# A mixture-of-experts kernel on one core: x loaded in float32 by SyncE and cast on the engines, instead of partly cast by Pool's transfer

## The chip, the cores and the metric

The kernel runs on one core of one Trainium2 chip. A core has five engines with their own instruction streams: TensorE (PE; its weight loads are listed as PEld), VectorE (DVE), ScalarE (ACT), GpSimd (POOL) and SyncE (SP). They share an on-chip memory of 128 partitions (SBUF) and the accumulators that TensorE writes (PSUM). Sixteen DMA engines move data between the chip's main memory and SBUF; an instruction on SP's or Pool's queue starts a transfer. The engines wait for one another, and for transfers, through semaphores. The metric is device time in microseconds (us).

## The reference

```python
n_experts, capacity, hidden, expert_hidden = 8, 256, 512, 2048

def reference(x, w1, w2):          # x 8x256x512, w1 8x512x2048, w2 8x2048x512, all float32
    h = np.matmul(x, w1)
    h = np.maximum(h, 0)
    return np.matmul(h, w2).astype(np.float32)
```

Eight experts, each with two matrix products and a ReLU between them. The weights are 67.1 MB in float32, x and the output 4.2 MB each.

## The kernel before

All products are done in bfloat16. The weights are cast while they are loaded: a transfer on Pool's queue reads float32 and writes bfloat16. Four experts' weights fit into SBUF (`w1_sb` and `w2_sb`, four slots each; expert e uses slot e mod 4).

*Loading x.* x is seen as 128 partitions with 16 rows of 512 numbers each: partition 16e + pp holds rows 16pp to 16pp + 15 of expert e. `x_sb`, in bfloat16, lies in slot 2 of `w2_sb`, which no expert needs yet. Rows 0 to 3 of each partition (`HEAD = 4`) are loaded by SP in float32 into the place of the outputs (`out_sb`, free until the first expert is done) and cast into `x_sb` by VectorE (L213 and L214). Rows 4 to 15 are loaded by Pool's first transfer (L153), which casts on the way. After L136 stands the end of a section of the program (L137, L138), where the engines meet; SP's first transfer is issued ahead of it.

*Transposing.* TensorE needs x with the hidden dimension on the partitions. It waits for the cast, for the identity matrix that Pool builds (L154 and L157) and for Pool's part of x (L323 to L325), and transposes 64 blocks of 128 x 128 in four rounds (`transposes`). VectorE and ScalarE copy each round from PSUM into `xT` (L206).

*Pool's queue.* After x and the identity come twelve loads of weights (L190) in the order of `loads`: w1 of experts 0 and 1, w2 of 0 and 1, w1 of 2 and 3, w2 of 2 and 3, and so on, with single experts and halves at the end. The first three are issued at once. The fourth overwrites slot 2, where x lies, and waits for the last transpose (L171). The later ones wait until the expert that had the slot has been computed (L174, L176). The last load is preceded by a tiny transfer into `out` (L181), whose landing tells Pool that the queue has come as far as the last weights; then the outputs of experts 0 to 6 are written by one transfer (L193), and SP writes those of expert 7 (L145). The semaphore `d_pool` counts 16 for x, 16 for the tiny transfer and 16 for the outputs.

*Computing.* SP waits for each load in turn and passes the news to TensorE (L142, L143). For each expert TensorE computes the hidden layer in four groups of 16 matmuls (`h_ps`), ScalarE applies ReLU into `hT` (L239), TensorE computes the outputs (`o_ps`, 32 matmuls), and VectorE copies them to `out_sb` (L225); the last half of expert 7 is copied by ScalarE (L245). TensorE's matmuls all go through one helper and are listed with L275.

Of the kernel before, what the change touches and what calls it, by code (L numbers as in the profile page):

```python
# [16 lines left out]
def kernel(  # L17
# [7 lines left out]
    nc = tc.nc  # L25
    P = 128
    E, C, H = x.shape
    F = w1.shape[2]
    MC = C // P
# [2 lines left out]

    R = E * C // P

    HEAD = 4

    NS = 4

# [10 lines left out]
    x_v = x.rearrange("e (pp r) k -> (e pp) (r k)", r=R)  # L49
# [7 lines left out]
    def allot(name, shape, dtype):  # L57
        nonlocal free
        places[name] = free
        t = nc.alloc_sbuf_tensor_at(name, shape, dtype, offset=free)  # L60
        free += math.prod(shape[1:]) * mybir.dt.size(dtype)
        return t


    out_sb = allot("out_sb", [P, E, MC, H], FP32)
# [7 lines left out]
    x_sb = w2_sb[:, 2, :]  # L73
# [8 lines left out]
    def sem(name):  # L82
        s = nc.alloc_semaphore(name)
        sems.append(s)
        return s

    d_last, d_pool = sem("d_last"), sem("d_pool")
# [3 lines left out]
        for w, slots in [(1, (0, 2, 3)), (2, (0, 1, 2, 3))]  # L91
        for i in slots
    }
    d_head, d_half = sem("d_head"), sem("d_half")
    s_event, s_cast, s_stored = sem("s_event"), sem("s_cast"), sem("s_stored")
    s_pe, v_last = sem("s_pe"), sem("v_last")

# [3 lines left out]
    def after_transposes(n):  # L101
        return s_pe, n

    def after_hidden(e, groups):
        return s_pe, K1 * MC + e * (NG + MC) + groups

    def after_outputs(e, halves):
        return s_pe, K1 * MC + e * (NG + MC) + NG + halves
# [22 lines left out]

    x_head = out_sb[:, :HEAD // MC].rearrange("p e m h -> p (e m h)")
    with tc.tile_critical(no_gpsimd_drain=True):
        nc.sync.dma_start(x_head, x_v[:, :HEAD * H]).then_inc(d_head, 16)  # L136
    tc.close()  # L137
    tc.compile()  # L138

# [1 line left out]
    for i, (w, es, h, n) in enumerate(loads):  # L141
# [8 lines left out]


    pool = nc.gpsimd
    pool.dma_start(x_sb[:, HEAD * H:], x_v[:, HEAD * H:]).then_inc(d_pool, 16)  # L153
    pool.memset(identity[:], 0.0).then_inc(s_event)  # L154
    pool.wait_ge(s_event, 1)

# [6 lines left out]
        pattern=[[-1, P]],  # L163
        channel_multiplier=1,
    ).then_inc(s_event)
    for i, (w, es, h, n) in enumerate(loads):


        old = es[-1] - NS
        if w == 2 and 2 in es:  # L170
            pool.wait_ge(*after_transposes(K1 * MC))  # L171
        if old >= 0 and h == 0:
            if w == 1:
                pool.wait_ge(*after_hidden(old, NG))  # L174
            else:
                pool.wait_ge(*after_outputs(old, MC))  # L176
        if i == len(loads) - 1:


            pool.wait_ge(s_event, 3)  # L180
            pool.dma_start(  # L181
                out_v[:16, 0, :16], out_sb[:16, 0, 0, :16]
            ).then_inc(d_pool, 16)
        e, ne, at_slot = es[0], len(es), es[0] % NS
        if w == 2:
            src = w2_v[:, e:e + ne, h:h + n, :].rearrange("p e h n -> p e (h n)")
            dst = w2_sb[:, at_slot:at_slot + ne, h * JH * H:(h + n) * JH * H]
        else:
            src, dst = w1_v[:, e:e + ne, :], w1_sb[:, at_slot:at_slot + ne, :]
        pool.dma_start(dst, src).then_inc(landed[i][0], 16)  # L190
    pool.wait_ge(s_event, 4)
    pool.wait_ge(d_pool, 32)
    pool.dma_start(  # L193
        out_v[:, :E - 1, :], out_sb[:, :E - 1].rearrange("p e m h -> p e (m h)")
    ).then_inc(d_pool, 16)
    pool.wait_ge(s_stored, 1)
    pool.wait_ge(d_pool, 48)
    used = [s.num for s in sems[1:]]
    used = range(min(used), max(used) + 1)
    pool.dma_reset(used)  # L200
# [9 lines left out]


    dve = nc.vector
    dve.wait_ge(d_head, 16)  # L213
    dve.tensor_copy(x_sb[:, :HEAD * H], x_head).then_inc(s_cast)  # L214
    dve.sem_inc(c_xt[0], 1)
    for ko in range(K1):
        dve.wait_ge(*after_transposes(ko * MC + 1))
# [11 lines left out]


    act = nc.scalar
    act.sem_inc(c_xt[1], 1)
    for ko in range(K1):
        act.wait_ge(*after_transposes(ko * MC + 2))
# [15 lines left out]
    pe = nc.tensor  # L250
# [42 lines left out]
    def last_column(step):  # L293

        return (P - 1) * step * 2
# [24 lines left out]
                i += 1  # L320
            t.then_inc(s_pe)

    pe.wait_ge(s_cast, 1)  # L323
    pe.wait_ge(s_event, 2)
    pe.wait_ge(d_pool, 16)  # L325
    x_first = X_AT + last_column(K1)
    pe.reg_mov(reg["x"], x_first)
    loop("transposes", reg["x"], x_first + K1 * 2, transposes)
# [146 lines left out]
```

## Time and profile before

| | |
|---|---|
| runs | 179.47 us median of 3 (179.31 to 180.14) |
| the profiled execution | 180.34 us in all, span 179.0 us |
| mean granted TensorE clock | 0.941 |
| read from main memory, written | 71.30 MB, 4.20 MB |
| transfers on Pool's queue | 38.80 MB at the destination |
| transfers on SP's queue | 1.57 MB |

The span goes from the first to the last instruction of one profiled execution; its own time in all is a little longer. In the lists, "x16" is a number of instructions, an arrow `a<-b` reads "a is written from b", times are in microseconds from the start of the span (the first number is the start, the second the length), and the bracket at the end tells how long the engine had been idle and what ended that. Bytes are counted at the destination, so a transfer that casts float32 to bfloat16 counts half of what it reads. The letter q after an engine's name marks its instruction queue, where transfers are issued and semaphores awaited. Transfers are listed with the time from issue to landing, that is, until the semaphore has its full count.

### The profile page before, as it was taken

How to read it: one execution, taken by the hardware profiler on the slowest of the kernel's cores; microseconds unless marked ns; L12 is line 12 of the kernel's file. 1: busy time of each engine (PE TensorE's matmuls, PEld its weight loads, DVE VectorE, ACT ScalarE, POOL GpSimd, SP SyncE). 2: the span in 40 equal slices, each digit the busy share in tenths (PEclk: the TensorE clock that was granted, in tenths of full speed). 3: DMA queues.
4: the chain of work that ended last, by engine and by line, in shares of the span. 5: the costliest groups of instructions: out<-in, count | busy, mean ns of one | idle time of the engine just before them, and what ended most of it. 6: DMA issues, size and time to landing. Idle time of an engine off the chain costs nothing. (4 is left out here: it accounts for less than half of the span.)

```text
span 179.0 us, 2075 instructions
## 1 busy us (share of the span) xinstructions
PE 126.7 (71%) x824; PEld 89.7 (50%) x832; DVE 15.8 (9%) x20; ACT 38.7 (22%) x38; POOL 10.9 (6%) x21
## 2 busy tenths in 40 slices
PE   0007630695029999993059999999999999959980
PEld 0006520585014695593023795695596497449530
DVE  0203420000000200200000200200110020020010
ACT  2002420044000063044000062053044044005310
POOL 3600010000000002101000101100020000001000
PEclk9999999999557999999657999999999999999999
DMA  5999989999999999999999998999999999999997
GB/s 185 253 207 231 227 190 231 227 194 223 231 209 205 227 216 201 231 216 198 231 220 194 231 223 190 231 227 194 223 231 205 209 234 216 198 212 218 303 421 310
DMA packets 3744, 40.37 MB, mean 226 GB/s; under 512 B 288, under 2 KB 288, under 8 KB 1312
## 3 DMA queue, kind: packets, MB, share of 16 engines
q0 software_dynamic: 3456, 38.80, 97.5%
q1 hardware_dynamic: 288, 1.57, 2.4%
HBM read 71.30 MB, written 4.20 MB: 422 GB/s over the span
## 5 line engine op out<-in xcount | busy, mean ns | idle before, releaser
L275 PE MATMUL o_ps<-w_sb,hT 128*128 x248 | 59.8, 396 | 19.6 <-PEq L99 18.8
L275 PE MATMUL h_ps<-xT,w_sb 128*128 x512 | 60.9, 281 | 11.3 <-PEq L99 11.3
L275 PEld LDWEIGHTS h_ps<-xT,w_sb 128*128 x512 | 57.7, 146 | 15.4 <-issue 12.0
L239 ACT ACTIVATE hT<-h_ps 128x1024 bf16<-128x1024 f32 x32 | 32.8, 1024 | 110.2 <-PE h_ps L275 110.2
L275 PEld LDWEIGHTS o_ps<-w_sb,hT 128*128 128x128 bf16 x256 | 25.5, 101 | 51.2 <-issue 24.7
L225 DVE COPY out_sb<-o_ps 128x512 f32<-128x512 f32 x15 | 9.7, 686 | 140.3 <-PE o_ps L275 140.3
L275 PE MATMUL xt_ps<-identity,w_sb 128*128 128x128 bf16 x64 | 7.6, 311 | 16.2 <-PEq L99 16.2
L275 PEld LDWEIGHTS xt_ps<-identity,w_sb 128*128 x64 | 6.5, 146 | 16.9 <-issue 16.9
L190 POOL DMA_DIRECT2D w_sb<-in_w_dram x12 | 8.0, 667 | 104.2 <-PE h_ps L275 56.9
L206 ACT COPY xT<-xt_ps 128x1024 bf16<-128x1024 bf16 x4 | 4.0, 1012 | 17.0 <-PE xt_ps L275 17.0
L206 DVE COPY xT<-xt_ps 128x1024 bf16<-128x1024 bf16 x4 | 4.9, 1224 | 12.2 <-PE xt_ps L275 12.2
L193 POOL DMA_DIRECT2D out_dram<-out_sb x1 | 1.0, 964 | 33.2 <-DMA out_dram<-out_sb 33.2
L245 ACT COPY out_sb<-o_ps 128x512 f32<-128x512 f32 x1 | 0.6, 586 | 5.9 <-PE o_ps L275 5.9
L206 ACT ACT_TABLE_LOAD x1 | 1.3, 1283 | 2.4 <-PEq L138 2.4
L214 DVE CAST w_sb<-out_sb 128x2048 bf16<-128x2048 f32 x1 | 1.2, 1227 | 5.8 <-DMA out_sb<-in_x_dram 5.8
L181 POOL DMA_DIRECT2D out_dram<-out_sb x1 | 0.5, 512 | 14.7 <-DVEq L228 14.7
L153 POOL DMA_DIRECT2D w_sb<-in_x_dram x1 | 0.7, 682 | 2.4 <-POOLq L138 2.4
L157 POOL TENSOR_SCALAR_AFFINE_SELECT identity<-identity 128x128 bf16<-128x128 bf16 x1 | 0.3, 284 | 0.2 <-POOL identity L154 0.2
L154 POOL MEMSET identity<- 128x128 bf16 x1 | 0.2, 224 | 0.0
L459 POOL MEMSET const-float32-0.0<- 128x1 f32 x1 | 0.1, 93 | 0.2 <-issue 0.2
L459 POOL MEMSET const-bfloat16-1.0<- 128x1 bf16 x1 | 0.1, 96 | 0.0
L459 POOL MEMSET const-uint8-127<- 128x1 uint8 x1 | 0.1, 96 | 0.0
(1 smaller groups left out, 0.1 us busy)
## 6 DMA issues: line engine op xcount, KB each, us to landing
w_sb<-in_w_dram POOLq DMA_DIRECT2D x5, 4096.0 KB, 47.1
w_sb<-in_w_dram POOLq DMA_DIRECT2D x5, 2048.0 KB, 51.2
out_dram<-out_sb POOLq DMA_DIRECT2D x1, 3584.0 KB, 12.9
w_sb<-in_w_dram POOLq DMA_DIRECT2D x2, 1024.0 KB, 43.3
w_sb<-in_x_dram POOLq DMA_DIRECT2D x1, 1536.0 KB, 10.6
out_sb<-in_x_dram SPq DMA_DIRECT2D x1, 1024.0 KB, 4.9
out_dram<-out_sb SPq DMA_DIRECT2D x1, 512.0 KB, 4.7
out_dram<-out_sb POOLq DMA_DIRECT2D x1, 1.0 KB, 33.7
```

Source lines behind the costliest of these rows:

```text
L153: pool.dma_start(x_sb[:, HEAD * H:], x_v[:, HEAD * H:]).then_inc(d_pool, 16)
L157: pool.affine_select(out=identity[:], in_=identity[:], compare_op=mybir.AluOpType.not_equal, fill=1.0, base=0, pattern=[[-1, P]], channel_ ...
L181: pool.dma_start(out_v[:16, 0, :16], out_sb[:16, 0, 0, :16]).then_inc(d_pool, 16)
L190: pool.dma_start(dst, src).then_inc(landed[i][0], 16)
L193: pool.dma_start(out_v[:, :E - 1, :], out_sb[:, :E - 1].rearrange("p e m h -> p e (m h)")).then_inc(d_pool, 16)
L206: return copy(xT[:, ko, m].rearrange("k (ep r2) -> k ep r2", r2=R // MC), xt_ps[m][:].rearrange("k r2 ep -> k ep r2"),)
L214: dve.tensor_copy(x_sb[:, :HEAD * H], x_head).then_inc(s_cast)
L225: cp = dve.tensor_copy(out_sb[:, e, m, :], o_ps[m][:])
L239: act.activation(hT[:, g * GJ:(g + 1) * GJ, :].rearrange("p a c -> p (a c)"), h_ps[g % UG][:], mybir.ActivationFunctionType.Relu,).then_in ...
L245: act.copy(out_sb[:, E - 1, 1, :], o_ps[1][:]).then_inc(v_last)
L275: return pe.add_instruction(inst)
L459: nc = _bacc.Bacc("TRN2", target_bir_lowering=False, num_devices=1)
```

## The change

Now SP loads all of x in float32, in three transfers (rows 0 to 3, 4 to 9 and 10 to 15 of each partition), into the place of the outputs, which they fill entirely. VectorE casts the first transfer, the second, and rows 10 to 13 of the third; ScalarE casts rows 14 and 15. Pool's transfer of x is gone; Pool builds the identity and then waits for x's second transfer before it issues the first weights. TensorE waits for four casts instead of one cast and Pool's transfer. `d_pool` counts 16 less.

```diff
-    HEAD = 4
+    HEAD, BODY = 4, 10
...
-    d_head, d_half = sem("d_head"), sem("d_half")
+    d_x, d_half = [sem(f"d_x{i}") for i in range(3)], sem("d_half")
...
-    x_head = out_sb[:, :HEAD // MC].rearrange("p e m h -> p (e m h)")
+    x_f32 = out_sb[:].rearrange("p e m h -> p (e m h)")
+
+    def rows(a, b):
+        return slice(a * H, b * H)
+
     with tc.tile_critical(no_gpsimd_drain=True):
-        nc.sync.dma_start(x_head, x_v[:, :HEAD * H]).then_inc(d_head, 16)
+        for i, (a, b) in enumerate([(0, HEAD), (HEAD, BODY), (BODY, R)]):
+            nc.sync.dma_start(x_f32[:, rows(a, b)], x_v[:, rows(a, b)]).then_inc(d_x[i], 16)
...
     pool = nc.gpsimd
-    pool.dma_start(x_sb[:, HEAD * H:], x_v[:, HEAD * H:]).then_inc(d_pool, 16)
     pool.memset(identity[:], 0.0).then_inc(s_event)
...
+    pool.wait_ge(d_x[1], 16)
     for i, (w, es, h, n) in enumerate(loads):
...
-    pool.wait_ge(d_pool, 32)
+    pool.wait_ge(d_pool, 16)
...
-    pool.wait_ge(d_pool, 48)
+    pool.wait_ge(d_pool, 32)
...
     dve = nc.vector
-    dve.wait_ge(d_head, 16)
-    dve.tensor_copy(x_sb[:, :HEAD * H], x_head).then_inc(s_cast)
+    SPLIT = 14
+
+    def cast(copy, a, b):
+        return copy(x_sb[:, rows(a, b)], x_f32[:, rows(a, b)])
+
+    dve.wait_ge(d_x[0], 16)
+    cast(dve.tensor_copy, 0, HEAD).then_inc(s_cast)
+    dve.wait_ge(d_x[1], 16)
+    cast(dve.tensor_copy, HEAD, BODY).then_inc(s_cast)
+    dve.wait_ge(d_x[2], 16)
+    cast(dve.tensor_copy, BODY, SPLIT).then_inc(s_cast)
...
     act = nc.scalar
+    act.wait_ge(d_x[2], 16)
+    cast(act.copy, SPLIT, R).then_inc(s_cast)
...
-    pe.wait_ge(s_cast, 1)
     pe.wait_ge(s_event, 2)
-    pe.wait_ge(d_pool, 16)
+    pe.wait_ge(s_cast, 4)
```

## The prediction

> **What bounds the kernel now.** First I read the page's busy shares against its slices. The last line below is the busy share of the 16 DMA engines in 40 slices.
>
> ```profile
> span 179.0 us, 2075 instructions
> PE 126.7 (71%) x824; PEld 89.7 (50%) x832; DVE 15.8 (9%) x20; ACT 38.7 (22%) x38; POOL 10.9 (6%) x21
> DMA  5999989999999999999999998999999999999997
> ```
>
> TensorE is idle 29% of the span, while the DMA engines are full from the first slice to the last. So the kernel is one stream of bytes, and the question is what one byte costs in each part of it. The table by stretches says that (last columns: granted clock, DMA share, GB/s arriving at the destination):
>
> ```profile
> 3.00:4.00 1.00, 0.00 (x0) 0.00 (x0) 0.00 (x0) 0.69 (x1) 0.76 (x3) 1.00 0.99 418
> 4.00:5.00 1.00, 0.00 (x0) 0.00 (x0) 0.00 (x0) 0.00 (x0) 0.85 (x2) 1.00 1.16 438
> ...
> 16.00:160.00 144.00, 111.16 (x719) 78.64 (x727) 12.94 (x18) 32.61 (x32) 5.71 (x10) 0.93 1.02 216
> ...
> 169.00:175.00 6.00, 4.67 (x22) 1.94 (x20) 0.69 (x1) 0.59 (x1) 0.00 (x0) 1.00 1.03 423
> 175.00:177.00 2.00, 0.00 (x0) 0.00 (x0) 0.00 (x0) 0.00 (x0) 0.00 (x0) 1.00 1.03 422
> ```
>
> The weights are cast on the way, so 216 GB/s arriving as bfloat16 are 432 GB/s read as float32. SP's plain float32 load of x (3 to 5 us) moves 428, the plain float32 output at the end 423. A float32 byte of the source therefore costs the same, cast or not. Next, the end, from the timeline, with the issues and their time to landing:
>
> ```profile
> 159.41 7.31 PE L275 MATMUL h_ps<-xT,w_sb 128*128 x64 [2.08 <-PEq L99]
> ...
> 166.61 7.07 PE L275 MATMUL o_ps<-w_sb,hT 128*128 x31
> ...
> 173.71 0.59 ACT L245 COPY out_sb<-o_ps 128x512 f32<-128x512 f32 x1 [5.93 <-PE o_ps L275]
> 174.32 0.35 SPq L145 DMA_DIRECT2D out_dram<-out_sb  x1
> ```
>
> ```profile
> out_dram<-out_sb POOLq DMA_DIRECT2D x1, 3584.0 KB, 12.9
> w_sb<-in_x_dram POOLq DMA_DIRECT2D x1, 1536.0 KB, 10.6
> out_sb<-in_x_dram SPq DMA_DIRECT2D x1, 1024.0 KB, 4.9
> out_dram<-out_sb SPq DMA_DIRECT2D x1, 512.0 KB, 4.7
> ```
>
> TensorE waits 2.08 us for the last expert's w1 before its last two stages; from there to the end everything follows the stream, and Pool's outputs (3584 KB, queued behind the last weights) keep the engines full until SP's last 512 KB land. So a microsecond by which the weights' stream starts later is a microsecond at the end, and a microsecond saved on x's computation is nothing. The change touches the first 14 us:
>
> ```profile
> 0.95 0.38 SPq L136 DMA_DIRECT2D out_sb<-in_x_dram  x1
> 2.41 1.28 ACT L206 ACT_TABLE_LOAD   x1 [2.41 <-PEq L138]
> 2.83 0.68 POOL L153 DMA_DIRECT2D w_sb<-in_x_dram  x1 [2.38 <-POOLq L138]
> 3.51 0.22 POOL L154 MEMSET identity<- 128x128 bf16 x1
> 3.97 0.28 POOL L157 TENSOR_SCALAR_AFFINE_SELECT identity<-identity 128x128 bf16<-128x128 bf16 x1 [0.24 <-POOL identity L154]
> 4.41 0.75 POOL L190 DMA_DIRECT2D w_sb<-in_w_dram  x1 [0.15 <-issue]
> 5.15 2.05 POOL L190 DMA_DIRECT2D w_sb<-in_w_dram  x2
> 5.83 1.23 DVE L214 CAST w_sb<-out_sb 128x2048 bf16<-128x2048 f32 x1 [5.83 <-DMA out_sb<-in_x_dram]
> 13.94 1.31 PEld L275 LDWEIGHTS xt_ps<-identity,w_sb 128*128 x13 [13.94 <-issue]
> ```
>
> Two moments are needed more finely, when Pool's x and when the weights begin to move:
>
> ```profile
> 4.60:4.80 0.20, 0.00 (x0) 0.00 (x0) 0.00 (x0) 0.00 (x0) 0.20 (x1) 1.00 0.78 328
> 4.80:5.00 0.20, 0.00 (x0) 0.00 (x0) 0.00 (x0) 0.00 (x0) 0.20 (x1) 1.00 1.95 553
> ...
> 12.20:12.40 0.20, 0.00 (x0) 0.00 (x0) 0.00 (x0) 0.00 (x0) 0.00 (x0) 1.00 0.68 143
> 12.40:12.60 0.20, 0.00 (x0) 0.00 (x0) 0.00 (x0) 0.00 (x0) 0.00 (x0) 1.00 3.51 737
> ```
>
> Packets come in bursts here. Pool's first x packets show at 4.80, where the share leaves 1 and nearly doubles: 1.97 us after its issue began and 1.3 us after it ended (2.83 + 0.68 = 3.51). By 12.5 the next larger burst is the first of w1; it stands right behind x in Pool's queue, so nothing is lost there.
>
> **The change part by part.**
>
> *SP's issues.* The first stays at 0.95. Two more of 0.38 us each put SP 0.76 us later at the barrier of L138, which releases ScalarE at 2.41 and Pool at 2.83, so these go to 3.2 and 3.6 at most. Pool then needs about 0.9 us for the identity, and waits for x until 9.5 (below). Hidden: 0. Without that cover it would be 0.76.
>
> *The bytes of x.* Four rows of 16 (1.05 MB) already come this way and land at 5.83, where VectorE starts. The other twelve (3.15 MB) take 3.15/0.428 = 7.35 us as float32; through Pool they took from about 5.1 to 12.5, 7.4 us. Gain 0.05, taken as 0; with 418 and 438 for the rate it is -0.1 to +0.2. Rows 4 to 10 take 3.67 us and land at 5.83 + 3.67 = 9.50, the last six at 13.18 (before 2.83 + 10.6 = 13.43). Their data end some 0.7 us ahead of the landing (x's head moved until about 5.1), at about 12.45: until then the engines are busy.
>
> *Pool's new wait.* This is the term that counts. Behind it stand all the weights: the first issue can't begin before 9.50, where it stood ready at 4.41. What covers it is the third x transfer, to 12.45. If it starts at once, data flow 2.0 us after the wait, at 11.6, and the cost is 0. But VectorE wakes on the same semaphore and casts six rows. The trace shows what a cast does to an issue beside it:
>
> ```profile
> 5.86:5.88 0.02, 0.02 (x2) 1.00 0.00 0
> ...
> L190 POOL DMA_DIRECT2D w_sb<-in_w_dram x12: 528/555/1333, 4.4 to 131.1; - x12
> ```
>
> Of the two issues that begin at 5.15 one ends at 5.87 (0.72 us), and the next, beside the cast that runs to 7.06, takes 1.33 us, the longest of all twelve, and ends at 7.20, which is 0.14 us after the cast. I read it as held by the cast, its last step done when VectorE lets go. The six-row cast has 3072 elements a partition: 1.23 x 1.5 = 1.84 us, 9.50 to 11.34. The first issue then ends at 11.48, and its data start 1.3 us later, at 12.8; by the end of x's burst instead of its start (about 5.4 instead of 4.80) 1.9 us later, at 13.4. Against 12.5 before that is +0.3 to +0.9. I take +0.4, near the lower end, because at 4.80 the first packets are surely there. Both ends, and 0 for no hold, stay for the range.
>
> The Trainium skill ("SBUF — State Buffer", section "Who interferes with whom") states the same as a rule that speaks against this change: a VectorE copy or cast in a two-port mode keeps GpSimd off the pair of ports they share for the whole instruction, and so off writing descriptors, and who begins first wins. The 1.33 us agree; by the rule, with Pool first, the cost would be 0 and the cast would wait instead. Its page "DMA: Bandwidth & Descriptors" (section "Specifications") gives a first byte about 1 us after a software-path issue; the row here has 1.97. By that figure the weights would move at 12.5 even when held, and the sum would be 0.
>
> *The casts and TensorE.* VectorE's last four rows take the 1.23 us of the old cast, 13.18 to 14.41; ScalarE's two rows (1024 elements) about the 1.01 us of a copy of that size below, to 14.2. The transposes start at about 14.5 instead of 13.94. What stands behind them:
>
> ```profile
> 23.76 1.01 ACT L206 COPY xT<-xt_ps 128x1024 bf16<-128x1024 bf16 x1 [1.61 <-PE xt_ps L275]
> 24.03 0.72 POOL L190 DMA_DIRECT2D w_sb<-in_w_dram  x1 [16.82 <-PE xt_ps L275]
> 32.93 9.89 PE L275 MATMUL h_ps<-xT,w_sb 128*128 x64 [9.21 <-PEq L99]
> ```
>
> The last copy ends at 24.77 and the first expert waits for its weights until 32.93, 8.2 us of cover. Pool's fourth issue, released by the transposes, goes from 24.0 to 24.6; the three issues before it hold 12.6 MB, 58 us at 216 GB/s. Cost 0. Even a table load (1.28) moved behind ScalarE's new wait, or a third transfer that shares the engines with weights and lands 2 us late, stays inside.
>
> *The sum.* 0 + 0 + 0.4 + 0: the span goes from 179.0 to 179.4. That execution took 180.34 in all, 1.34 beside its span, so it becomes 180.74, a ratio of 1.002. The median of the runs is 179.47, 0.87 below that execution; 179.47 x 1.002 = 179.9.
>
> **The rivals.**
>
> *Pool isn't held* (it gets its descriptors out before the cast, or the 1.33 had another reason). For it: the issue at 5.15 needs only 0.72 and both engines wake together. Against it: the end 0.14 us after the cast. Then the weights are ready at 11.6, under x's third transfer, and what is left is the -0.2 to +0.1 of x's bytes: 179.3 to 179.6.
>
> *The whole issue comes after the cast* (slower). A cold Pool that wakes behind VectorE may have nothing prepared: 11.34 + 0.75 (an unhindered issue) + 1.3 to 1.9 = 13.4 to 14.0, +0.9 to +1.5, 180.4 to 181.0. For it: unlike the held issue of the trace, which followed others, this one is the first of its kind in the kernel. Against it: that one ended 0.14 us after the cast. It decides from the point where the weights' first burst comes after 13.4, x's bytes being done.
>
> *Two queues move more than one* (faster). If Pool isn't held and weights run beside x from 11.6 at no cost to it, up to 0.8 us of stream is saved, with the 0.2 of the best rate 1.0: 178.5. Against it: at the end, when SP's 512 KB run beside Pool's outputs, the rate is 422, before that 423.
>
> **How the numbers follow.** Forecast (held, +0.2 to +0.9) 0.48; not held 0.24; whole issue behind the cast 0.18; faster 0.10. About 0.5% (0.9 us: 178.6 and 180.4) is what a measurement of this kernel can tell from no change. Within it lie the not-held case and 0.42 of the forecast, 0.66 together; slower are the third case and 0.06 of the forecast's upper edge, 0.24; faster 0.10. The range runs from 179.0, below the not-held case, to 181.0, the dearest case with a price; the faster case and some chance beyond both ends are left out.
>
> **What would show it.** In the changed profile: x's second landing at about 9.5 (the start of VectorE's second cast); a first weight issue of some 2 us that ends 0.1 to 0.2 us after that cast; a dip in GB/s between 12.4 and 12.9; transposes from 14.5; the first expert's matmuls at 33.3 instead of 32.93, and every later wait for weights shifted by the same 0.4. The forecast is wrong if the first weights land no later than before, or over 0.9 us later, or if the shift at 33 isn't the shift at the end.

## The result and the profile after

| | kernel before | changed kernel |
|---|---|---|
| runs | 179.59 us median of 7 (179.31 to 180.14) | 180.72 us median of 7 (180.25 to 181.82) |
| profiled execution, span | 180.34 us, 179.0 us | 180.25 us, 178.9 us |

The ratio is 1.0066, with a 95% interval from 1.0042 to 1.0089: the changed kernel is slower by 0.7%, 1.1 us. The two profiled executions don't show that difference: the one of before was 0.75 us above its median, the one of the changed kernel was the fastest of its seven. So the spans can't be subtracted; one has to read where in each trace time is lost.

The page and the timeline of the changed kernel's first 15 us, and the rows for its first weights (the line with "DMA to landing" gives the shortest, median and longest time from issue to landing of the twelve loads; the shortest is that of the first):

```profile
span 178.9 us, 2079 instructions
...
DMA  5999999999999999999999999999999999999997
```

```profile
0.95 1.33 SPq L142 DMA_DIRECT2D out_sb<-in_x_dram  x3
...
3.29 1.28 ACT L222 ACT_TABLE_LOAD   x1 [3.29 <-PEq L144]
...
5.71 1.23 DVE L222 CAST w_sb<-out_sb 128x2048 bf16<-128x2048 f32 x1 [5.71 <-DMA out_sb<-in_x_dram]
9.38 1.76 DVE L222 CAST w_sb<-out_sb 128x3072 bf16<-128x3072 f32 x1 [2.44 <-DMA out_sb<-in_x_dram]
9.64 1.64 POOL L196 DMA_DIRECT2D w_sb<-in_w_dram  x1 [5.63 <-DMA out_sb<-in_x_dram]
...
13.05 1.23 DVE L222 CAST w_sb<-out_sb 128x2048 bf16<-128x2048 f32 x1 [1.92 <-DMA out_sb<-in_x_dram]
14.84 1.63 PEld L292 LDWEIGHTS xt_ps<-identity,w_sb 128*128 x16 [14.84 <-issue]
...
33.49 7.78 PE L292 MATMUL h_ps<-xT,w_sb 128*128 x55 [8.88 <-PEq L99]
```

```profile
L196 POOL DMA_DIRECT2D w_sb<-in_w_dram x12: 531/560/1637, 9.6 to 130.2; - x12
...
DMA to landing us min/median/max: 23.7/50.0/66.5
```

x arrives as it should: its three transfers wake VectorE at 5.71, 9.38 and 13.05. Pool's first issue takes 1.64 us and ends at 11.28, 0.14 after the cast beside it (9.38 + 1.76 = 11.14). The first weights land at 9.64 + 23.7 = 33.3. For the kernel before the same row is

```profile
DMA to landing us min/median/max: 28.4/49.8/67.2
```

so 4.41 + 28.4 = 32.8: the stream of weights is 0.5 us late. At the other end of the trace:

```profile
159.37 8.97 PE L292 MATMUL h_ps<-xT,w_sb 128*128 x64 [2.66 <-PEq L99]
...
168.22 7.07 PE L292 MATMUL o_ps<-w_sb,hT 128*128 x31
...
175.94 0.35 SPq L151 DMA_DIRECT2D out_dram<-out_sb  x1
```

```profile
out_dram<-out_sb SPq DMA_DIRECT2D x1, 512.0 KB, 3.0
```

Here TensorE waits for the last w1 until 159.37, the same moment as in the first trace of before. Two things are therefore in play: a later start, and something that the kernel before loses on the way and this one, in this run, doesn't. TensorE's last hidden layer takes 8.97 us instead of 7.31, since part of it runs at half clock after a wait of 2.66 us (first column after the engines' busy times: granted clock; before, then changed):

```profile
160.00:161.00 1.00, 1.00 (x12) 1.00 (x11) 0.00 (x0) 0.00 (x0) 0.00 (x0) 1.00 0.90 188
```

```profile
160.00:161.00 1.00, 1.00 (x6) 0.80 (x5) 0.00 (x0) 0.00 (x0) 0.00 (x0) 0.50 1.05 221
```

That looks costly, but SP's last output, issued 1.6 us later, lands 3.0 us after its issue instead of 4.7.

### The profile page after: what moved, and what is told of

Same layout as the page of the kernel before. It is cut to its first block, busy times and chain, and to the rows that moved or that the text cites. A ratio compares the mean times of both kernels' runs of the same rounds, so it can differ in the third digit from the quotient of the medians.

```text
span 178.9 us, 2079 instructions
## 1 busy us (share of the span) xinstructions
PE 126.7 (71%) x824; PEld 89.7 (50%) x832; DVE 18.8 (11%) x22; ACT 39.7 (22%) x39; POOL 10.4 (6%) x20
## 5 line engine op out<-in xcount | busy, mean ns | idle before, releaser
L256 ACT ACTIVATE hT<-h_ps 128x1024 bf16<-128x1024 f32 x32 | 32.8, 1024 | 111.0 <-PE h_ps L292 111.0
L222 DVE CAST w_sb<-out_sb 128x2048 bf16<-128x2048 f32 (+1 forms) x3 | 4.2, 1405 | 10.1 <-DMA out_sb<-in_x_dram 10.1
L222 ACT CAST w_sb<-out_sb 128x1024 bf16<-128x1024 f32 x1 | 1.0, 1046 | 8.5 <-DMA out_sb<-in_x_dram 8.5
L187 POOL DMA_DIRECT2D out_dram<-out_sb x1 | 0.5, 512 | 14.7 <-DVEq L243 14.7
```

The lines of the kernel that those rows point to most:

```text
L187: pool.dma_start(out_v[:16, 0, :16], out_sb[:16, 0, 0, :16]).then_inc(d_pool, 16)
L222: return copy(x_sb[:, rows(a, b)], x_f32[:, rows(a, b)])
L256: act.activation(hT[:, g * GJ:(g + 1) * GJ, :].rearrange("p a c -> p (a c)"), h_ps[g % UG][:], mybir.ActivationFunctionType.Relu,).then_in ...
```

## The experiments

Every kernel ran beside the kernel before on the same chip. The kernel before had medians of 180.08, 179.81, 179.66 and 179.76 us in the four groups, with single runs from 179.18 to 181.0, so ratios carry that spread and medians are given beside them.

### The two kernels again

The kernel before, unchanged. 

> The kernel before, unchanged, for the spread of its runs and a second trace. In the first trace the loads of 4 MB that follow the first one land 19.53, 19.57, 19.40 and 19.49 us after one another, and the execution took 180.34 us, 0.75 more than the median of 179.59. In the changed kernel's trace the same steps are 19.38, 19.32, 19.35, 19.35. If the pace of the stream is a property of the run (theory of the late start: the change costs the 0.57 us by which the first weights land later, 33.33 against 32.76, and the first trace of before hid it by a slow pace), a typical run of before has steps near 19.4, lands its last weights near 168.4 and takes 179.3 to 179.8 us. If the pace is a property of the kernel (rival: x through Pool slows what follows), the steps are near 19.5 again and the time is above 180.

The changed kernel, unchanged. 

> The changed kernel, unchanged, for a second trace of it. Theory of the late start: the first weights land at 33.2 to 33.5 again, and a run at the median (180.7 us, span 179.4) has them no later, but later steps of the stream or a slower last stage of TensorE. Rival, a start that varies: the first weights land between 33.3 and 34.5, as the run's time does. Rival, the clock: runs in which TensorE's last 64 hidden matmuls fall under half clock (8.97 us instead of 7.31) are the slow ones.

Measured: before 179.86 us, ratio 0.9988 [0.9967, 1.0009]; changed 181.05 us, 1.0045 [1.0029, 1.0062]. The rows of the first weights, before and changed:

```profile
L190 POOL DMA_DIRECT2D w_sb<-in_w_dram x12: 531/555/1291, 4.4 to 131.0; - x12
...
DMA to landing us min/median/max: 28.1/49.6/67.2
```

```profile
L196 POOL DMA_DIRECT2D w_sb<-in_w_dram x12: 528/566/1635, 9.9 to 131.3; - x12
...
DMA to landing us min/median/max: 24.1/49.7/66.9
```

That is 32.5 against 34.0: the late start varies, from 0.5 to 1.5 us. In the second trace of before the steps from one 4 MB load to the next were 19.53, 19.56, 19.40 and 19.39 us, as in its first, so the expectation that its pace was an accident of the first trace failed: it is slower than the 19.35 of the changed kernel, in both traces. The late start isn't the whole difference; the kernel before has a loss of its own.

### No wait on Pool

```diff
-    pool.wait_ge(d_x[1], 16)
```

> The changed kernel without Pool's wait for x's second transfer, so that the weights are issued at about 4.4 us and move beside x. Theory of the late start: no idle time at 12 to 14 us, the weights' stream gives up only the 4.2 MB of x, the first weights land at 32.6 to 32.9, ratio to the kernel before 0.998 to 1.002. x lands later, at 15 to 18 us, and the transposes end by 29, which costs nothing. Rival (three hardware-queue transfers beside the weights, or the float32 bytes themselves, cost the time): the ratio stays at 1.005 to 1.008.

Measured: 179.41 us, ratio 0.9957 [0.9940, 0.9973].

```profile
L195 POOL DMA_DIRECT2D w_sb<-in_w_dram x12: 528/564/1411, 4.2 to 130.3; - x12
...
DMA to landing us min/median/max: 28.3/49.0/65.5
```

One of its twelve runs took 468.33 us, which nothing on record explains; the ratio is that of the other eleven (179.34 to 179.54). The first weights land at 32.5, and the kernel is 1.6 us faster than the changed one in the same group: that is the price of the wait. It is also faster than the kernel before, beyond what was expected. x's last rows land only at 26.5 beside the weights, and that costs nothing.

### Is it the cast beside the issue?

```diff
-    dve.wait_ge(d_x[1], 16)
-    cast(dve.tensor_copy, HEAD, BODY).then_inc(s_cast)
     dve.wait_ge(d_x[2], 16)
+    cast(dve.tensor_copy, HEAD, BODY).then_inc(s_cast)
     cast(dve.tensor_copy, BODY, SPLIT).then_inc(s_cast)
```

> The changed kernel with VectorE's second cast (rows 4 to 9) put off until x's third transfer has landed, so that no cast runs beside Pool's first issue. Theory that the cast holds the issue: the first issue takes 0.7 to 0.8 us instead of 1.64 and ends near 10.4, its data start by 11.7, under x's third transfer, the first weights land at 32.6 to 32.9, and the ratio is 0.998 to 1.002; the transposes start 1.8 us later, at 16.6, at no cost. Rival (the issue is slow because it is the first on Pool's queue): it still takes over 1.3 us, and the first weights land at 33.2 or later, ratio 1.004 to 1.008.

Measured: 181.09 us, ratio 1.0046 [1.0025, 1.0068].

```profile
9.73 0.87 POOL L196 DMA_DIRECT2D w_sb<-in_w_dram  x1 [5.72 <-DMA out_sb<-in_x_dram]
...
13.14 2.90 DVE L222 CAST w_sb<-out_sb 128x3072 bf16<-128x3072 f32 x2 [6.12 <-DMA out_sb<-in_x_dram]
```

```profile
L196 POOL DMA_DIRECT2D w_sb<-in_w_dram x12: 528/563/867, 9.7 to 131.6; - x12
...
DMA to landing us min/median/max: 24.5/49.5/65.6
```

The cast does hold the issue: without it the issue takes 0.87 us instead of 1.64 and ends at 10.60. But the first weights land at 34.2, no earlier than with it, and the time is the same. What is lost is lost between the issue and the flow of data. The slope of the DMA shares says where. In the stretch from 12.8 to 13.8, where x's data are through (kernel before, changed kernel, then this one; last two columns: DMA share, GB/s):

```profile
12.80:13.80 1.00, 0.00 (x0) 0.00 (x0) 0.00 (x0) 0.00 (x0) 0.00 (x0) 1.00 0.77 164
```

```profile
12.80:13.80 1.00, 0.00 (x0) 0.00 (x0) 0.75 (x1) 0.75 (x1) 0.00 (x0) 1.00 0.61 115
```

```profile
12.80:13.80 1.00, 0.00 (x0) 0.00 (x0) 0.66 (x1) 0.66 (x1) 0.00 (x0) 1.00 0.87 98
```

The share counts the packets' time, the rate their bytes. In the steady stream of before (the prediction's row from 16 to 160 us) it is 1.02 for 216 GB/s, 0.0047 for each GB/s, and in this stretch of before it is the same. In the other two rows it is 0.0053 and 0.0089: the packets of weights that start in this stretch take 1.1 and 1.9 times as long as later ones.

Since two more casts ran at 13 us here, a second try took VectorE out altogether:

```diff
-    dve.wait_ge(d_x[1], 16)
-    cast(dve.tensor_copy, HEAD, BODY).then_inc(s_cast)
-    dve.wait_ge(d_x[2], 16)
-    cast(dve.tensor_copy, BODY, SPLIT).then_inc(s_cast)
...
+    act.wait_ge(d_x[1], 16)
     act.wait_ge(d_x[2], 16)
-    cast(act.copy, SPLIT, R).then_inc(s_cast)
+    cast(act.copy, HEAD, R).then_inc(s_cast)
...
-    pe.wait_ge(s_cast, 4)
+    pe.wait_ge(s_cast, 2)
```

> The changed kernel with rows 4 to 15 cast by ScalarE alone in one instruction after x's third transfer, so that VectorE does nothing from 7 to 18 us, neither beside Pool's issue nor beside the first packets of weights. Theory A (any start of Pool's queue with nothing of x left to cover it is slow): the issue takes 0.7 to 0.9 us, the first packets of the weights still up to 1.6 to 2.7 us instead of 1.23, the first weights land at 33.0 to 34.3, ratio 1.002 to 1.007. Theory B (VectorE's casts at 13 us slow the first packets): they take 1.23 to 1.35, the first weights land at 32.4 to 32.8, ratio 0.995 to 0.999. The transposes start near 19 in both, which is covered.

Measured: 181.19 us, ratio 1.0082 [1.0060, 1.0104], a little above what Theory A expected. The issue takes 0.87 us, and the first weights land at 9.8 + 23.6 = 33.4 (in the shortest of the seven runs, 180.33 us):

```profile
9.78 0.87 POOL L196 DMA_DIRECT2D w_sb<-in_w_dram  x1 [5.77 <-DMA out_sb<-in_x_dram]
```

```profile
L196 POOL DMA_DIRECT2D w_sb<-in_w_dram x12: 528/563/867, 9.8 to 130.3; - x12
...
DMA to landing us min/median/max: 23.6/49.9/60.7
```

Theory B falls: with no cast anywhere near, the first sixteen packets of weights still take 1.58 us in the mean instead of 1.23. VectorE is not the cause. Nor is it Pool issuing its next loads at the same moment: in both kernels of this section the third issue has ended (12.02 and 12.08) before the first packet of weights starts (12.28 and 12.20).

### Is it the queue's first use?

```diff
+    pool.dma_start(w1_sb[:16, 0, :16], w1_v[:16, 0, :16]).then_inc(d_pool, 16)
     pool.memset(identity[:], 0.0).then_inc(s_event)
...
+    pool.wait_ge(d_pool, 16)
     pool.wait_ge(d_x[1], 16)
```

The two later counts of `d_pool` rise by 16. 

> The changed kernel with a transfer of 16 x 16 numbers (into a place that the first weights overwrite) as the first of Pool's queue, landed long before the weights are issued. If the slow first packets are the price of the queue's first use, they take 1.23 to 1.3 us here, the first weights land at 32.6 to 33.0 and the ratio is 0.997 to 1.001. If any start from an idle queue is slow, the first packets still take up to 2 us and more, the first weights land at 33.2 to 34.2 and the ratio is 1.003 to 1.007.

Measured: 180.85 us, ratio 1.0046 [1.0027, 1.0065]; the tiny transfer landed at 9.3, the first weights at 10.0 + 23.5 = 33.5, and their first sixteen packets took 1.76 us in the mean. Not the queue's first use, then.

### How much of x has to be left

With an earlier release, more of x is left to move while the weights' transfer starts. Four doses: Pool waits for the first transfer, or the second transfer ends at another row.

```diff
-    pool.wait_ge(d_x[1], 16)
+    pool.wait_ge(d_x[0], 16)
```

> The changed kernel, but Pool waits for x's first transfer (5.8 us) instead of the second (9.4). Theory of the cold start: from Pool's release to a full flow of weights it takes 3.5 to 4.5 us whether a cast holds the issue or not, and in the changed kernel only 3.1 us of x are left to cover it; here 6.6 us are left, so the start is covered, the first weights land at 32.5 to 32.8 and the ratio to the kernel before is 0.995 to 0.998, as without any wait. Rival (any wait for x on Pool costs what it costs): the ratio stays at 1.003 to 1.007.

```diff
-    HEAD, BODY = 4, 10
+    HEAD, BODY = 4, 7
```

> The changed kernel with the second transfer up to row 6 (BODY = 7), so that Pool is released at 7.6 and 4.9 us of x are left. Theory of the cold start: 4.9 is more than the 3.5 to 4.5 it takes, so the start is covered: first weights 32.5 to 32.9, ratio 0.995 to 0.999. Rival: 33.3 to 34.2, ratio 1.003 to 1.007.

```diff
-    HEAD, BODY = 4, 10
+    HEAD, BODY = 4, 8
```

> The changed kernel with BODY = 8: Pool is released at 8.2, the first issue, held by a cast of four rows, ends near 9.7, and x's data end at 12.5 as always, 2.8 us after that. It brackets the cover that a start of Pool's queue needs: with 3.7 us (BODY = 7, issue end 8.8) the first packets were as quick as any, with 1.9 us (issue end 10.6) not. If 2.8 is enough, the first packets take 1.23 us, the first weights land at 32.3 to 32.6 and the time is 179.2 to 179.5; if not, the first packets take over 1.4 us and the first weights land at 32.8 to 33.6, time 179.7 to 180.8.

```diff
-    HEAD, BODY = 4, 10
+    HEAD, BODY = 4, 12
```

> The changed kernel with the second transfer up to row 11 instead of 9 (BODY = 12), so that Pool is released at 10.6 instead of 9.4 and only 1.8 us of x are left. Theory of the cold start: the 1.2 us come on top, the first weights land at 34.4 to 35.6, ratio 1.010 to 1.016. Rival (the loss has nothing to do with how much of x is left): 33.3 to 34.2 and 1.003 to 1.007 again.

Measured, with the end of Pool's first issue and, from the records of the DMA packets, the first sixteen packets of weights (one on each engine):

```
                        issue   first 16 packets       first weights   median    ratio to the kernel before
                        ends    mean us   longest us   land            us
wait for transfer 1      7.1     1.23      1.23        32.4            179.36    0.9972 [0.9960, 0.9984]
BODY = 7                 8.8     1.23      1.23        32.4            179.32    0.9972 [0.9955, 0.9989]
BODY = 8                 9.7     1.39      1.83        33.0            179.88    1.0009 [0.9994, 1.0024]
BODY = 10 (changed)     11.3     1.58      1.99        33.3            180.72    1.0066 [1.0042, 1.0089]
BODY = 10 (again)       11.5     1.78      2.21        34.0            181.05    1.0045 [1.0029, 1.0062]
BODY = 12               13.1     1.70      1.94        34.6            181.46    1.0084 [1.0060, 1.0107]
```

x's data are through at about 12.5 where no weights move beside them. They do move beside x in the first two rows: with BODY = 7 the first packet of weights starts at 11.9, x's last one ends at 13.9, and its landing wakes VectorE only at 15.46:

```profile
7.92 0.87 POOL L196 DMA_DIRECT2D w_sb<-in_w_dram  x1 [3.92 <-DMA out_sb<-in_x_dram]
...
15.46 2.03 DVE L222 CAST w_sb<-out_sb 128x3584 bf16<-128x3584 f32 x1 [6.85 <-DMA out_sb<-in_x_dram]
```

Counted to 12.5, an issue that ends 3.7 us ahead is covered, one that ends 2.8 us ahead isn't quite, one that ends 1.2 us ahead costs 0.9 to 1.6 us at the landing. Between these the price doesn't fall evenly: the two kernels with the issue free of the cast end it 1.9 us ahead and pay 1.8 and 1.0 us. With BODY = 12 the engines stand still before the first packet, and the slope after it is 0.0065 (1.70 for 262 GB/s), 1.4 times the steady one:

```profile
12.80:13.80 1.00, 0.00 (x0) 0.00 (x0) 0.82 (x2) 0.64 (x1) 1.00 (x2) 1.00 0.00 0
...
13.80:14.80 1.00, 0.04 (x1) 0.05 (x2) 0.05 (x1) 0.40 (x1) 0.92 (x2) 1.00 1.70 262
```

Its first issue ran beside a cast of eight rows and ended 0.15 us after it:

```profile
10.69 2.29 DVE L222 CAST w_sb<-out_sb 128x4096 bf16<-128x4096 f32 x1 [3.63 <-DMA out_sb<-in_x_dram]
10.96 2.17 POOL L196 DMA_DIRECT2D w_sb<-in_w_dram  x1 [6.95 <-DMA out_sb<-in_x_dram]
```

With BODY = 12 the landing was in the expected range, the ratio below it: the expectation put the added delay on the changed kernel's mean and forgot that the kernel before is itself above the 179.3 of a covered start. BODY = 8 landed where its second branch said, in landing and time; the mean of its first packets, 1.39 us, stayed just under the 1.4 expected there.

### The same stop in the kernel before

```diff
+    pool.wait_ge(d_pool, 16)
     for i, (w, es, h, n) in enumerate(loads):
```

> The kernel before, with Pool waiting for its own transfer of x (landing at 13.2 to 13.4) before it issues the weights. Nothing is left in flight and no cast runs. Theory A: the issue ends near 14.3, the weights flow fully some 1.7 us later, at 15.8 to 16.2, and the first weights land at 35.5 to 36.2, 3.0 to 3.5 later than in the kernel before; if a late start goes to the end one to one, the time is 182.5 to 183.5, ratio 1.016 to 1.020. Rival (a shift is partly made up later): under 1.012.

Measured: 182.68 us, ratio 1.0161 [1.0132, 1.0190].

```profile
L191 POOL DMA_DIRECT2D w_sb<-in_w_dram x12: 531/555/748, 13.9 to 133.9; - x12
...
DMA to landing us min/median/max: 22.2/49.7/69.9
```

With no cast beside the issue and nothing on SP's queue, the first packets are slow again (1.69 us in the mean), and 13.9 + 22.2 = 36.1 is the latest landing of all. Theory A's landing, time and ratio hold; the issue ended at 14.7 instead of 14.3.

### Where the kernel before loses

```diff
-        for i, (a, b) in enumerate([(0, HEAD), (HEAD, BODY), (BODY, R)]):
+        for i, (a, b) in enumerate([(0, HEAD)]):
...
+    for i, (a, b) in enumerate([(HEAD, BODY), (BODY, R)]):
+        pool.dma_start(x_f32[:, rows(a, b)], x_v[:, rows(a, b)]).then_inc(d_x[i + 1], 16)
     pool.memset(identity[:], 0.0).then_inc(s_event)
...
-    pool.wait_ge(d_x[1], 16)
```

> The changed kernel with x's second and third transfers, still in float32, on Pool's queue directly ahead of the weights, and no wait. It asks where the kernel before loses what those with SP's three transfers and early weights (179.3 to 179.4) don't: its traces show packets of 1.25 to 1.36 us instead of 1.23 between 40 and 110 us, and its runs spread from 179.3 to 181. If x on Pool's queue leads to that (through the order in which the engines finish), this kernel shows such packets too, spreads over 0.7 us or more and has a ratio of 0.998 to 1.002. If the cast of x in the transfer leads to it, there are none, the runs lie within 0.3 us and the ratio is 0.995 to 0.998. Theory A expects no slow first packets in either case, since the queue never runs empty.

Measured: 179.95 us, ratio 1.0015 [0.9994, 1.0035], single runs from 179.37 to 181.03. It is the first branch by ratio and spread: with x on Pool's queue the runs scatter like those of before, cast or not, while eleven of twelve runs with BODY = 7 lie between 179.23 and 179.46. The profiled run of this kernel was one of its shortest (span 178.1) and has only 14 packets of weights above 1.24 us after 30 us, against 145 and 137 in the two traces of before. The second trace of the changed kernel has 142, too, so x on Pool's queue isn't the only way to them. What sets them off stays open.

### All traces in one row

The landing of the first weights is the first issue's start plus the shortest time to landing; what is left goes from there to the end of the span.

| kernel | first weights land | span | rest |
|---|---|---|---|
| before, two traces | 32.8, 32.5 | 179.0, 178.7 | 146.2, 146.2 |
| changed, two traces | 33.3, 34.0 | 178.9, 180.0 | 145.6, 146.0 |
| no wait | 32.5 | 178.1 | 145.6 |
| wait for transfer 1, BODY = 7 | 32.4, 32.4 | 178.0, 178.0 | 145.6, 145.6 |
| BODY = 8 | 33.0 | 178.6 | 145.6 |
| x in float32 on Pool's queue | 32.4 | 178.1 | 145.7 |
| BODY = 12 | 34.6 | 180.2 | 145.6 |
| late cast, no VectorE cast | 34.2, 33.4 | 179.9, 179.0 | 145.7, 145.6 |
| before, with the stop | 36.1 | 181.7 | 145.6 |
| tiny transfer first | 33.5 | 179.7 | 146.2 |

From a landing at 32.4 to one at 36.1 the rest is 145.6 or 145.7: a late start goes to the end one to one. The traces with 146.0 and 146.2 are those with over fifty slow packets after 30 us. The changed kernel's first trace has TensorE's last hidden layer at half clock (8.97 us), BODY = 12 at full clock (7.32), and both have 145.6, so the clock costs nothing here.

## Why the prediction was right or wrong

The range held (180.72 in 179.0 to 181.0), but the forecast, no change beyond 0.5% at 179.9, was not what happened: the time is that of the second rival, whose mechanism (the whole issue done after the cast) isn't the cause either. That the range held is luck: it reached up to 181.0 only for that rival. By the prediction's own signs the forecast was wrong: in the first pair of traces the first expert's matmuls begin 0.56 us later (33.49 against 32.93) but the end doesn't (178.9 against 179.0), and in the second pair the first weights land 1.5 us later.

- **The bound, and one to one to the end.** Right. The DMA engines are full throughout, and the rest after the first landing is constant while the start moves by 3.7 us.
- **x's bytes, SP's issues, the casts and TensorE.** Right, within 0.35 us: x landed at 9.4 and 13.0 (9.50 and 13.18 forecast), ScalarE's table load began at 3.29 (3.2), the transposes at 14.84 (14.5), and the cover behind them was not used up. Even transposes from 20.7 us on, in the kernel without VectorE's casts, cost nothing there.
- **The hold.** Right as a row: 1.64 us, ended 0.14 us after the cast; the first issue beside a longer cast (2.29 us, BODY = 12) took 2.17. The rule that the Trainium skill gives ("SBUF — State Buffer", section "Who interferes with whom"), that whoever begins first keeps the other waiting for the whole instruction, agrees with it: the two casts began 0.26 and 0.27 us before the issues. Wrong as the price: without the hold (0.87 us) the time was 181.09, with it 181.05.
- **The step that failed** is "the first issue then ends at 11.48, and its data start 1.3 us later, at 12.8", with the sentence before it that, if the issue starts at once, "the cost is 0". The start itself came true (12.66 in the mean of the first sixteen packets); what failed is to take a start for the flow, which is what I did with the first packets of Pool's x at 4.80. What the runs showed in its place: with the engines empty (BODY = 12 and the stop in the kernel before) it takes 3.0 us from the end of the issue until the last of the first sixteen packets is through and the weights flow at full pace, unless enough of another transfer is left to keep the engines busy; single first packets took up to 2.2 us (2.75 without the hold). The term sized +0.4 measured 0.5 and 1.5 us at the first landing against the two traces of before, and 0.9 and 1.6 us against a covered start. Cover alone isn't the whole account: Pool's x in the kernel before also started as SP's data ran out (by 5.5, its issue had ended at 3.51), and its first packets were only a little slow, 1.06 us in the mean instead of 0.93. Why that start was so mild, and what makes the packets slow, stays open.
- **The rival of no hold** (179.3 to 179.6) fell: when the hold was taken away, nothing was won. By the 1 us that the Trainium skill's page "DMA: Bandwidth & Descriptors" gives as a first byte (section "Specifications") the cost would have been 0. With empty engines the first packets do begin about that soon after the end of the issue (1.0 us in the mean with BODY = 12 and with the stop; the 1.97 that the prediction set beside it counts from the issue's start), but they are not yet the flow.
- **What no step had.** The kernel before, in its two traces, loses some 0.5 us on the way (rest 146.2 against 145.6), which the prediction took as part of the stream's pace. A kernel that loads x as the change does, but releases Pool early enough, doesn't in eleven of twelve runs: 179.32 against 179.81 in the median. The change thus gave up 0.9 to 1.6 us at the start and won back some of 0.5; the measured 1.1 fits that. That win was argued nowhere in the prediction.

The version that beats both is the changed kernel with BODY = 7: 179.32 us, 0.9972 of the kernel before [0.9955, 0.9989], or without Pool's wait, 179.41, 0.9957 [0.9940, 0.9973].

## What to carry to other kernels

Where a kernel is one stream of transfers, don't price a handover from one queue to another by when its first packet appears; price it by when the flow is full, and look whether the trace that you take the number from had other work to cover it. A wait put ahead of a stream's first transfer must come several microseconds before the engines run dry, here between 2.8 and 3.7 us before, counted from the end of the issue. And when two traces of equal span come from kernels of unequal medians, compare them milestone by milestone: a landing and the rest after it told apart what the spans hid.

## What was not expected of the hardware

- The first packets of a load of weights on Pool's queue that starts alone take 1.6 to 2.0 us in the mean instead of 1.23 (longest 2.75), on a used queue as on a fresh one, and with VectorE idle. When they begin beside SP's data they take 1.23.
- While SP's transfers fill the engines, a transfer on Pool's queue is slow to get its turn: its first packet starts 3.1 to 3.3 us after the end of its issue in all four traces where SP's data last that long (8.2 without the wait, 10.4 with the wait for transfer 1, 11.9 with BODY = 7, 7.7 for the tiny transfer), against 0.7 and 0.8 us with empty engines. From there the two share the engines: without the wait x's third transfer lands at 26.5 instead of 13.0.
- In some runs packets in the middle of the stream take up to 1.36 us instead of 1.23, on many engines, for tens of microseconds. Why the late cast's first packets (1.96 us in the mean, although the issue ended 0.7 us earlier) were slower than the changed kernel's, and what brings on the slow packets in mid-stream, wasn't settled.
